# A head sum as two fp32r products, a later start for the last conv block, and output tiles finished one by one, in a one-core hybrid block

## The chip, the core and the metric

The kernel runs on one core of one Trainium2 chip, as one launch. The metric is the device time of that core in microseconds (us). The engines are TensorE (PE in the profile, with its weight loads as PEld), VectorE (DVE), ScalarE (ACT), GpSimd (POOL) and the DMA queues that SyncE (SP) starts. All arithmetic is in float32 or in fp32r, a rounded float32 format in which TensorE multiplies. An exact float32 operand is turned into two fp32r ones: a rounded copy ("hi") and the rest ("lo" = value minus hi).

## The reference, cut to what matters

```
h = rmsnorm(x) * (1 + scale) + shift                 # x: 2048 rows of 1024
p = h @ w_in                                         # value, gate, r, k, v, low-rank parts, output gates
# branch A: u = val*sigmoid(gate); causal depthwise conv of width 31; layernorm; swish; * silu(gate); @ w_conv_out
# branch B (RWKV-7), 16 heads of 64:
kk = (k * k_k).reshape(heads)
kk = kk / max(sqrt(sum(kk * kk, axis=-1)), 1e-12)    # the head sum that the change touches
o  = delta_rule_scan(r, decay, k, v, kk, kk * a)
y_rwkv = (groupnorm(o) + bonus) * silu(og) @ w_rwkv_out
out = (sigmoid(g_conv)*y_conv + sigmoid(g_rwkv)*y_rwkv) @ w_out
result = rmsnorm(x + gate * out, final_g)            # the end that the change touches
```

## The kernel before, in words

**Two phases.** Channels lie on the 128 partitions and 512 positions on the free axis, so a tile is 128x512. The 2048 positions are four blocks (b = 0 to 3). In the first phase each block runs `project` for every 128 columns of `w_in`: eight steps of three fp32r products (hi by hi, hi by lo, lo by hi). Between the projections lie the small products of the RWKV recurrence. A block has four slots (`slot`, g = 0 to 3), each with two pairs of heads (`pair`, line 998): 4 blocks x 8 pairs = 32 calls.

In the second phase blocks are taken two at a time ("s" = 0 and 1, the last pair of blocks being s = 1). For each, `wino` (line 1895) runs three Strassen-like products, in the order ro (RWKV output), co (conv output), o (the last projection). So `wino` is called six times, and `turn[0]` counts the calls. Each has seven part products, of four column tiles and 12 matmuls a tile. The part products are taken in the order 0, 4, 6, 2, 1, 3, 5 (0, 1, 6, 4, 2, 3, 5 in the first).

**Who sets the order.** The program is written out under `manual_schedule`: generators (`Task`) yield a time at which they may go on, and `poll` (line 223) lets them go on, the lowest rank first, as the emitted matmuls move the planner's clock `now`. `note` holds the planner's costs and due times. `ok(t)` is the time at which a tile is ready. `burst` (line 287) adds a lag of LAG = 1.0 us to it before a product is put into TensorE's queue. `idle("DVE", AHEAD)` lets a task wait until VectorE's planned work is less than 0.7 us ahead. Each engine then works through its own instructions in that order, and semaphores hold an instruction whose operand is late.

**The head sum** (lines 1043 to 1051, in `pair`). ScalarE squares k times k_k into `sq` (float32); one float32 product with `bones` (ones in two 64x64 blocks) sums over each head; ScalarE copies it to `ssr`; SP stores two rows of it to `dN`. Further on in the same generator come `y`, `BK`, `KR` and the masked products `As`, which the group's triangular inverse starts from. `dn` (the inverse of the squared norm) is read back from `dN`. A like sum stands further on: `rk` is split into `rh` and `s_lo`, and two fp32r products with `bones` follow.

**The conv branch of the last block.** The first three blocks' conv branches are finished in the first phase. The last block's layer norm ends in `last_norm` (`side[1]`), and `last_u` (line 2109), a task of rank 2, then takes the eight tiles one after the other: load `y` and the gate `co`, multiply by the inverse deviation, two ACT functions, two DVE products, store to `u_d`. It starts once `side[1]` is done and four cells of `uc` are free. The loads for the last co product wait until all eight are stored (`more_["u"]`).

**Lending buffers.** `lend_cells` (line 2077) hands buffers of the first phase to the second. At its end it loads `final_g` as a broadcast row `fg` (128x1024), then lends four weight slots and two raw weight slots, and lets six weight loads run ahead.

**The end** (`final`, line 2167, for each o product). Four output tiles of 128 rows for each of two blocks, each in two halves (h_ = 0, 1). VectorE adds x to the PSUM sum; ScalarE squares with an accumulated row sum into `sq8` (`square`); `finish(b_, ns)` waits until both halves of the rows `ns` are there, then runs on columns: mean plus epsilon, an integer first guess of the inverse root and three Newton steps of three operations, 12 small DVE operations in all; then one DVE multiplication by `rs` and `fg` and one store for each half tile. Before, `finish` is called once for the four tiles of block 0 (`finish(0, [0, 1, 2, 3])`), and for block 1 once, or four times with one tile each in the last pair. The last halves come in the order: block 1 with part product 3, block 0 with part product 5, the last one. All squares of a pair write the one tile `sq8`, and `finish` waits for `ok(sq)`.

Of the kernel before, what the change touches and what calls it, by code (L numbers as in the profile page):

```python
# [9 lines left out]
F32 = mybir.dt.float32  # L10
# [8 lines left out]
P = 128  # L19
# [63 lines left out]
def hybrid_block(ctx: ExitStack, tc: tile.TileContext, x, x_t, vecs, convk, w2a2, final_g, ada, w_in, w_co, w_ro, w_o, crow, out,  # L83
# [169 lines left out]
    def ok(*aps):  # L253
        ks = [key(a) for a in aps]
        return lambda: max(ready[q] for q in ks)
# [8 lines left out]
    def when(f):  # L264
        return lambda: 0.0 if f() else None
# [21 lines left out]
    def burst(*ws):  # L287
        w = both(*ws)

        def f():  # L290
            r = w()
            if r is None:
                return r
            return r + lag[0]

        return f
# [701 lines left out]
    def pair(G, q_, box):  # L998
# [41 lines left out]
        E1x = E1[:, :, 0:CH].rearrange("p (c e) t -> p c e t", e=2)  # L1040
        E1i = E1[:, :, 1:].rearrange("p (c e) t -> p c e t", e=2)
        E24 = E2.rearrange("p (c e t) -> p c e t", e=2, t=CH)
        sq = e1.tile([P, TB], F32, name="sq", tag="sq")
        nc.scalar.activation(sq, k, AF.Square, scale=vc("rwkv_k_k", pr))
        yield burst(ok(sq), free, bank("aux"))
        pss = pa.tile([P, TB], F32, name="aux", tag="aux")
        nc.tensor.matmul(pss, bones.bitcast(F32), sq, start=True, stop=True)
        ssr = e1.tile([P, TB], F32, name="ssr", tag="sq")
        nc.scalar.copy(ssr, pss)
        yield ok(ssr)  # L1050
# [680 lines left out]
    with tc.manual_schedule():  # L1731
# [345 lines left out]
        def lend_cells():  # L2077
            yield when(lambda: Gs[-2].chained)
            l3_cells(sc, "As", "As", "tk", "tk", "KR", "KR")
            yield when(lambda: Gs[-2].normed)  # L2080
            l3_cells(sc, "uv")
            yield when(lambda: Gs[-1].chained)
            l3_cells(sc, "KR", "KR")
            l3_cells(oc, "As", "As", "tk", "tk")
            yield when(lambda: Gs[-1].normed)
            wide[0] = 8
            l3_cells(oc, "uv")
            yield both(when(lambda: groups_[-1].done and side[0].done and side[1].done and len(mr[1][1].got) == 4),
                       hx.room(HXB - 4))
            for _ in range(HXB - 4):  # L2090
                fc.add(hx.take("fc"))
            late.close()
            sp = more_["sp"] = ctx.enter_context(tc.tile_pool(name="sp", bufs=1, reuse_waits="tile"))
            more_["fg"] = sp.tile([P, D], F32, name="fg")
            nc.sync.dma_start(more_["fg"], final_g.unsqueeze(0).broadcast_to([P, D]))
            wr.free.extend([now[0]] * NWX)
            wr.slots.extend([lambda name: sp.tile([P, KT, P], F32R, name=name, tag="wx", bufs=NWX)] * NWX)
            for t_ in slices(sp.tile([P, NRAWX, TB], F32, name="w_raw")):
                raws.add(t_)
            depth[0] = WB  # L2100
# [6 lines left out]
                    to.add(*slices(e2.tile([P, TB], F32, name="fc", tag=tag_, bufs=n_)))  # L2107

        def last_u():
            yield when(lambda: side[1].done)  # L2110
            yield uc.room(4)
            rl = uc.take()
            nc.sync.dma_start(rl, rl_d)
# [53 lines left out]
        def final(b0):  # L2167
# [4 lines left out]
                             for h_, b_, n in order_])  # L2172
            have = {}
            sp, fg = more_["sp"], more_["fg"]
            sq = sp.tile([P, 2, 4, 2], F32, name="sq8", tag="sq8", bufs=2)

            def plus(h_, b_, n, t_, ps):
                f = order_.index((h_, b_, n))
# [6 lines left out]
            class Done:  # L2185
# [10 lines left out]

                def square(self, h_, b_, n, t_, home):
                    yield ok(t_)
                    fsq = sp.tile([P, TB], F32, name="fsq", tag="fsq", bufs=2)
                    nc.scalar.activation(fsq, t_, AF.Square, accum_out=sq[:, b_, n, h_:h_ + 1])  # L2200
                    have[b_, n, h_] = t_, home

            def finish(b_, ns):
                m = len(ns)
                yield when(lambda: all((b_, n, h_) in have for n in ns for h_ in range(2)))
                vs, rs, rt = [sp.tile([P, 4], F32, name=n_, tag=n_, bufs=2)[:, :m] for n_ in ("vs", "rs", "rt")]
                yield both(ok(sq), idle("DVE", AHEAD))
                s_ = sq[:, b_, ns[0]:ns[0] + m, :]
                nc.vector.tensor_tensor(out=vs, in0=s_[:, :, 0], in1=s_[:, :, 1], op=ALU.add)
                nc.vector.tensor_scalar(out=vs, in0=vs, scalar1=1.0 / D, scalar2=RMS_EPS, op0=ALU.mult, op1=ALU.add)  # L2210
                rsqrt(rs, vs, None, nc.vector, rt)
                for i, n in enumerate(ns):
                    t0 = (b0 + b_) * TB + n * P
                    for h_ in range(2):
                        t_, home = have[b_, n, h_]
                        yield both(ok(t_, rs), idle("DVE", AHEAD))
                        nc.vector.scalar_tensor_tensor(out=t_, in0=t_, scalar=rs[:, i:i + 1],
                                                       in1=fg[:, h_ * TB:h_ * TB + TB], op0=ALU.mult, op1=ALU.mult)
                        nc.sync.dma_start(out[t0:t0 + P, h_ * TB:h_ * TB + TB], t_)
                        home.give(t_)  # L2220

            Task(finish(0, [0, 1, 2, 3]), 2)
            for ns in ([[0], [1], [2], [3]] if last else [[0, 1, 2, 3]]):
                Task(finish(1, ns), 2)
            return sums8(held(), held(), held(), Done(), plus)

        for c_, (m, s_) in zip(todo, seq_):
# [49 lines left out]
```

## Time and profile before

| What | Value |
|---|---|
| Median of 3 runs | 2690.75 us (2689.71 to 2692.74) |
| Profiled execution, its own time | 2690.07 us |
| Span of the profile (first to last instruction) | 2688.4 us |
| Mean granted TensorE clock | 0.989 |
| Matmuls | 18324 |
| VectorE instructions | 3658 |
| ScalarE instructions | 2306 |
| GpSimd instructions | 1817 |
| DMA | 712.11 MB, mean 265 GB/s |

Busy time is the share of the span in which an engine has an instruction under way; for TensorE it is rough, since matmuls overlap and their ends are modelled. So its pace is read from the starts of successive matmuls, not from the length of one. In a timeline row the first number is the start, the second the length, then engine, line, operation, output<-inputs, sizes and count, and in brackets the idle time before it and what ended that. Because all instructions are recorded in one helper, every line number reads L194, and tile names tell the operations apart.

### The profile page before, as it was taken

The page shows a single profiled execution, that of the slowest core. Times are in us where ns is not written, and L with a number is a line of the kernel's source. Part 1 is how long each engine was busy: PE and PEld are TensorE (multiplying, and loading weights), DVE is VectorE, ACT ScalarE, POOL GpSimd, SP SyncE. Part 2 cuts the span into 40 slices and gives each one's busy share as a digit, 9 for nine tenths or more (in the row PEclk, how much of TensorE's full clock was granted, in tenths as well). Part 3 has the DMA queues.
Part 4 walks back from the last instruction along what each step waited for, and adds up shares of the span by engine and source line. Part 5 has one row for each costly group of instructions (what it writes and reads, how often), then busy time and mean ns, then how long its engine had stood idle before and what let it go on. Part 6 is the DMA issues. An engine that isn't in the chain of part 4 may idle for free.

```text
span 2688.4 us, 50710 instructions
## 1 busy us (share of the span) xinstructions
PE 2589.7 (96%) x18324; PEld 2086.4 (78%) x18324; DVE 2178.6 (81%) x3658; ACT 1188.6 (44%) x2306; POOL 1315.4 (49%) x1817
## 2 busy tenths in 40 slices
PE   6999999999999999999999998999999988899997
PEld 5877888777877888888888877877887766688886
DVE  6786889788879887978698877878888699888586
ACT  5544444443434434434444333434344454455443
POOL 0576758562658383827573756492726593000000
PEclk9999999999999999999999999999999999999998
DMA  9788778787787688967876888686766779789884
GB/s 352 271 300 308 263 264 284 261 299 242 245 270 242 223 286 275 312 206 272 279 254 224 293 262 259 216 307 204 273 185 213 254 267 308 241 310 332 306 266 167
DMA packets 390835, 712.11 MB, mean 265 GB/s; under 512 B 137508, under 2 KB 141944, under 8 KB 390584
## 3 DMA queue, kind: packets, MB, share of 16 engines
q1 hardware_dynamic: 390584, 708.87, 78.0%
q8 instruction: 144, 2.36, 0.4%
q14 instruction: 107, 0.88, 0.1%
HBM read 494.34 MB, written 213.26 MB: 263 GB/s over the span
## 4 chain that ended last, share of the span: by engine, by line
PE 78%; DVE 10%; DMA 5%; POOL 3%; issue 2%; SPq 2%; ACT 1%; DVEq 0%; POOLq 0%; ACTq 0%
PE ps_main L194 63%; PE aux L194 6%; PE xo L194 5%; PE late L194 3%; SPq L194 2%; DVE As L194 1%; DMA w_lo<-kl_in 1%; DVE acc L194 1%; PE ps_f L194 1%; DVE gst L194 1%; DMA As<-dT 1%; DVE rs_t L194 1%; DVE h_lo L194 1%; DVE S L194 1%; DMA gr_d<-th 0%
## 5 line engine op out<-in xcount | busy, mean ns | idle before, releaser
L194 PE MATMUL ps_main<-h_hi,w_hi 128*128 128x512 f32 x2304 | 923.6, 401 | 8.0 <-DVE lora L194 4.7
L194 PE MATMUL ps_main<-h_hi,w_lo 128*128 128x512 f32 x2304 | 925.2, 402 | 5.0 <-POOL w_lo L194 2.9
L194 PE MATMUL ps_main<-h_lo,w_hi 128*128 128x512 f32 x2304 | 923.0, 401 | 0.0
L194 DVE SCALAR_TENSOR_TENSOR acc<-u,ck,acc 128x512 f32<-128x512 f32 x928 | 698.6, 753 | 26.7
L194 PEld LDWEIGHTS ps_main<-h_hi,w_hi 128*128 128x128 f32 x2304 | 435.1, 189 | 105.4 <-issue 6.7
L194 PEld LDWEIGHTS ps_main<-h_hi,w_lo 128*128 128x128 f32 x2304 | 435.1, 189 | 101.8 <-issue 5.7
L194 PEld LDWEIGHTS ps_main<-h_lo,w_hi 128*128 128x128 f32 x2304 | 435.1, 189 | 92.5 <-issue 5.0
L194 PE MATMUL ps_main<-h_hi,w_c 128*128 128x512 f32 x896 | 292.3, 405 | 10.5 <-DVE mr L194 3.6
L194 POOL TENSOR_TENSOR itmp<-La,TT 128x126 f32<-128x126 f32 (+22 forms) x496 | 207.0, 417 | 46.3 <-issue 13.2
L194 ACT ACTIVATE th<-ps_main 128x512 f32<-128x512 f32 x160 | 95.6, 598 | 285.8 <-PE ps_main L194 264.7
L194 POOL TENSOR_TENSOR TT<-TT,itmp 128x126 f32<-128x126 f32 (+22 forms) x496 | 202.1, 407 | 38.9
L194 PEld LDWEIGHTS ps_main<-h_hi,w_c 128*128 128x128 f32 x896 | 172.7, 193 | 53.0 <-ACT h_hi L194 4.2
L194 POOL TENSOR_TENSOR w_lo<-w_st,w_hi 128x1024 fp32r<-128x1024 f32 x55 | 133.4, 2425 | 140.1 <-ACT w_hi L194 125.0
L194 PE MATMUL ps_main<-h_lo,w_c 128*128 128x512 f32 x448 | 182.4, 407 | 14.0 <-DVE h_lo L194 12.2
L194 ACT COPY uv<-xo 64x256 f32<-64x256 f32 (+1 forms) x192 | 80.9, 438 | 208.9 <-PE xo L194 153.8
L194 DVE SCALAR_TENSOR_TENSOR S<-xo,pe,Se 64x64 f32<-64x64 f32 x512 | 123.1, 280 | 49.2 <-PE xo L194 37.9
L194 ACT CAST w_c<-w_raw 128x512 fp32r<-128x512 f32 x168 | 102.3, 619 | 93.1 <-DMA w_raw<-wk_o 33.9
L194 PE MATMUL ps_main<-w_c,h_hi 128*128 128x512 f32 x448 | 140.3, 394 | 0.0
L194 DVE TENSOR_TENSOR As<-aux,maskA 128x512 f32<-128x512 f32 x128 | 82.3, 684 | 47.5 <-PE aux L194 46.9
L194 PEld LDWEIGHTS ps_main<-h_lo,w_c 128*128 128x128 f32 x448 | 86.8, 194 | 37.2 <-DVE h_lo L194 15.4
L194 ACT ACTIVATE Se<-S,pe 128x128 f32<-128x128 f32 x256 | 88.7, 395 | 40.0 <-DVE S L194 38.7
L194 ACT ACTIVATE t<-ps_main,mu 128x512 f32<-128x512 f32 x96 | 65.9, 686 | 80.0 <-PE ps_main L194 79.6
(294 smaller groups left out, 4508.7 us busy)
## 6 DMA issues: line engine op xcount, KB each, us to landing
w_hi<-kh_in SPq DMA_DIRECT2D x219, 512.0 KB
w_lo<-kl_in SPq DMA_DIRECT2D x219, 512.0 KB
w_st<-w_in_t SPq DMA_DIRECT2D x73, 512.0 KB
kh_in<-w_hi SPq DMA_DIRECT2D x71, 512.0 KB
kl_in<-w_lo SPq DMA_DIRECT2D x71, 512.0 KB
lny<-y_d SPq DMA_DIRECT2D x80, 256.0 KB
w_raw<-wk_o SPq DMA_DIRECT2D x56, 256.0 KB
ada_st<-ada_t SPq DMA_DIRECT2D x16, 512.0 KB
```

Of the source, the lines that this page charges most:

```text
L194: r = f(*a, **k)
```

## The change

**The head sum.** The square `sq` goes into another buffer; ScalarE makes a rounded copy `sqh` (fp32r); VectorE takes the rest `sql`; the one float32 product becomes two fp32r products with `bones`. **The conv branch.** `last_u` also waits until `turn[0] >= 2`, the call of the second `wino` (co of the first pair of blocks). **The end.** `fg` is multiplied once by -1/256 on ScalarE, and `lend_cells` waits for its load first. In the last pair each of the eight tiles has its own small square-sum tile and its own `finish`, with eight small operations in place of 12 (the constants are folded into `fg`). In the first pair the four tiles stay together, with one operation more. `finish` tasks of block 1 are put in ahead of block 0. `fsq` has one buffer in place of two.

```diff
@@ in pair
-        sq = e1.tile([P, TB], F32, name="sq", tag="sq")
+        sq = e1.tile([P, TB], F32, name="sq", tag=YT)
         nc.scalar.activation(sq, k, AF.Square, scale=vc("rwkv_k_k", pr))
-        yield burst(ok(sq), free, bank("aux"))
+        sqh = e1.tile([P, TB], F32R, name="sqh", tag="sq")
+        yield ok(sq)
+        nc.scalar.copy(sqh, sq)
+        sql = e1.tile([P, TB], F32R, name="sql", tag=RHT)
+        yield ok(sqh)
+        nc.vector.tensor_tensor(out=sql, in0=sq, in1=sqh.bitcast(F32), op=ALU.subtract)
+        yield burst(ok(sql), free, bank("aux"))
         pss = pa.tile([P, TB], F32, name="aux", tag="aux")
-        nc.tensor.matmul(pss, bones.bitcast(F32), sq, start=True, stop=True)
+        nc.tensor.matmul(pss, bones, sqh, start=True, stop=False)
+        nc.tensor.matmul(pss, bones, sql, start=False, stop=True)
@@ in lend_cells
             nc.sync.dma_start(more_["fg"], final_g.unsqueeze(0).broadcast_to([P, D]))
+            yield ok(more_["fg"])
+            nc.scalar.mul(more_["fg"], more_["fg"], -1.0 / 256)
             wr.free.extend([now[0]] * NWX)
@@ in last_u
-            yield when(lambda: side[1].done)
+            yield when(lambda: side[1].done and turn[0] >= 2)
@@ in final
-            sq = sp.tile([P, 2, 4, 2], F32, name="sq8", tag="sq8", bufs=2)
+            if last:
+                sq = [[sp.tile([P, 1, 2], F32, name="sqn", tag="sqn", bufs=8) for _ in range(4)] for _ in range(2)]
+            else:
+                s8 = sp.tile([P, 2, 4, 2], F32, name="sq8", tag="sq8", bufs=1)
+                sq = [[s8[:, b_, n:n + 1, :] for n in range(4)] for b_ in range(2)]
@@ in square
-                    fsq = sp.tile([P, TB], F32, name="fsq", tag="fsq", bufs=2)
-                    nc.scalar.activation(fsq, t_, AF.Square, accum_out=sq[:, b_, n, h_:h_ + 1])
+                    fsq = sp.tile([P, TB], F32, name="fsq", tag="fsq", bufs=1)
+                    nc.scalar.activation(fsq, t_, AF.Square, accum_out=sq[b_][n][:, 0, h_:h_ + 1])
@@ in finish
-                yield both(ok(sq), idle("DVE", AHEAD))
-                s_ = sq[:, b_, ns[0]:ns[0] + m, :]
-                nc.vector.tensor_tensor(out=vs, in0=s_[:, :, 0], in1=s_[:, :, 1], op=ALU.add)
-                nc.vector.tensor_scalar(out=vs, in0=vs, scalar1=1.0 / D, scalar2=RMS_EPS, op0=ALU.mult, op1=ALU.add)
-                rsqrt(rs, vs, None, nc.vector, rt)
+                yield both(ok(sq[b_][ns[0]]), idle("DVE", AHEAD))
+                s_ = s8[:, b_] if m > 1 else sq[b_][ns[0]]
+                if m > 1:
+                    nc.vector.tensor_tensor(out=vs, in0=s_[:, :, 0], in1=s_[:, :, 1], op=ALU.add)
+                    nc.vector.tensor_scalar(out=vs, in0=vs, scalar1=1.0 / D, scalar2=RMS_EPS, op0=ALU.mult, op1=ALU.add)
+                    rsqrt(rs, vs, None, nc.vector, rt)
+                    nc.vector.tensor_scalar(out=rs, in0=rs, scalar1=-256.0, scalar2=None, op0=ALU.mult)
+                else:
+                    nc.vector.tensor_scalar(out=vs, in0=s_[:, :, 0], scalar1=s_[:, 0, 1:2], scalar2=D * RMS_EPS, op0=ALU.add,
+                                            op1=ALU.add)
+                    nc.vector.tensor_scalar(out=rs.bitcast(I32), in0=vs.bitcast(I32), scalar1=-0.5, scalar2=float(0x5F3759DF),
+                                            op0=ALU.mult, op1=ALU.add)
+                    for z_ in (3.0, 12.0, 768.0):
+                        nc.vector.tensor_scalar(out=rt, in0=rs, scalar1=rs, scalar2=vs, op0=ALU.mult, op1=ALU.mult)
+                        nc.vector.tensor_scalar(out=rs, in0=rt, scalar1=z_, scalar2=rs, op0=ALU.subtract, op1=ALU.mult)
@@ at the end of final
-            Task(finish(0, [0, 1, 2, 3]), 2)
-            for ns in ([[0], [1], [2], [3]] if last else [[0, 1, 2, 3]]):
-                Task(finish(1, ns), 2)
+            for b_ in (1, 0):
+                for ns in ([[0], [1], [2], [3]] if last else [[0, 1, 2, 3]]):
+                    Task(finish(b_, ns), 2)
```

## The prediction, made before the change was run

> **What bounds the kernel now.** I read the page's busy times first, then its chain of work, then the busy time by stage.
>
> ```profile
> span 2688.4 us, 50710 instructions
> PE 2589.7 (96%) x18324; PEld 2086.4 (78%) x18324; DVE 2178.6 (81%) x3658; ACT 1188.6 (44%) x2306; POOL 1315.4 (49%) x1817
> PE 78%; DVE 10%; DMA 5%; POOL 3%; issue 2%; SPq 2%; ACT 1%; DVEq 0%; POOLq 0%; ACTq 0%
> ```
>
> TensorE is busy for 96% of the span and holds 78% of the chain that ends last. So an instruction taken from TensorE should shorten the span, if it lies where TensorE does not wait. The windows view tells where that is. Its columns: the window and its length, then busy us and instructions of PE, PEld, DVE, ACT and POOL, then clock, DMA share and GB/s.
>
> ```profile
> 56.00:600.00 544.00, 535.07 (x3714) 430.77 (x3715) 436.61 (x672) 267.18 (x485) 356.90 (x440) 0.99 0.81 281
> 600.00:1130.00 530.00, 525.05 (x4084) 424.42 (x4083) 445.52 (x752) 215.59 (x436) 298.96 (x433) 1.00 0.79 262
> 1130.00:1640.00 510.00, 504.20 (x3963) 408.45 (x3962) 411.11 (x697) 212.96 (x433) 291.94 (x453) 1.00 0.78 256
> 1640.00:2090.00 450.00, 439.90 (x3296) 354.03 (x3295) 371.45 (x613) 173.57 (x346) 246.24 (x358) 1.00 0.72 235
> 2090.00:2200.00 110.00, 101.44 (x1179) 80.22 (x1179) 87.27 (x159) 56.88 (x118) 76.64 (x98) 1.00 0.75 254
> 2200.00:2260.00 60.00, 48.24 (x226) 36.41 (x225) 52.47 (x78) 23.51 (x44) 41.15 (x28) 0.89 0.89 293
> 2260.00:2350.00 90.00, 79.70 (x329) 62.84 (x328) 78.80 (x129) 44.09 (x77) 0.00 (x0) 0.95 0.81 274
> 2673.00:2689.00 16.00, 0.00 (x0) 0.00 (x0) 11.37 (x36) 0.72 (x2) 0.00 (x0) 0.55 0.48 180
> ```
>
> The first four rows are the first phase. TensorE idles there for 8.9 + 5.0 + 5.8 + 10.1 = 29.8 us of 2034, or 1.5%: it is the bound. The next three rows are the handover between the phases: 8.6 + 11.8 + 10.3 = 30.7 us idle in 260, with VectorE busy for 87% in the second and 88% in the third; what binds there is VectorE, the loads and the order together. The last row is the tail: TensorE has nothing left and VectorE works alone. All 32 head sums lie in the first phase, `last_u` starts in the handover, and the single tiles lie in the tail.
>
> **The head sum.** Around one of the 32, the timeline of TensorE says:
>
> ```profile
> 2059.04 0.40 PE L194 MATMUL ps_main<-h_lo,w_hi 128*128 128x512 f32 x1
> 2059.28 1.02 PE L194 MATMUL aux<-sq,bones 128*128 128x512 f32 x2
> 2059.73 0.79 PE L194 MATMUL ps_main<-h_hi,w_lo 128*128 128x512 f32 x1
> 2060.36 0.39 PE L194 MATMUL ps_main<-h_hi,w_hi 128*128 128x512 f32 x1
> 2060.59 0.40 PE L194 MATMUL ps_main<-h_lo,w_hi 128*128 128x512 f32 x1
> ...
> 454.95 0.40 PE L194 MATMUL aux<-rh,bones 128*128 128x512 f32 x1
> 455.19 0.39 PE L194 MATMUL aux<-s_lo,bones 128*128 128x512 f32 x1
> 455.42 0.39 PE L194 MATMUL ps_main<-h_lo,w_hi 128*128 128x512 f32 x1
> ```
>
> Projections start 0.23 us apart (2060.36 to 2060.59). The float32 product is two records, and from its start to that of the second projection behind it 1.08 us pass (2059.28 to 2060.36), one projection included: 1.08 - 0.23 = 0.85 us. The new form is in the trace already: the two fp32r products of the other head sum, with the same ones matrix, take 455.42 - 454.95 = 0.47 us. Each head sum gives back 0.85 - 0.47 = 0.38 us, and 32 of them 12.2 us.
>
> Added are 32 rounded copies on ScalarE and 32 subtractions on VectorE. Their nearest rows (the list of groups; the last number before the bar is the count, behind it busy us and mean ns) and the ones that show how long such a VectorE operation can take:
>
> ```profile
> L194 ACT CAST rh<-rk 128x512 fp32r<-128x512 f32 x32 | 19.8, 618 | 51.4 <-DVE rk L194 51.3
> L194 DVE TENSOR_TENSOR h_lo<-mr,h_hi 128x512 fp32r<-128x512 f32 x40 | 26.7, 684 | 8.8 <-ACT h_hi L194 8.7
> L194 DVE TENSOR_TENSOR h_lo<-hf,h_hi 128x512 fp32r<-128x512 f32 x40 | 33.0, 854 | 7.9 <-ACT h_hi L194 7.7
> ...
> L194 DVE SCALAR_TENSOR_TENSOR y<-ta,k x32: 674/689/2425, 83.4 to 2060.2; 128x512 f32<-128x512 f32 x32
> ...
> PE aux L194 <- ACT sq L194: 0.5, 1, 0.5
> ```
>
> ScalarE gets 32 x 0.62 = 19.8 us, VectorE 32 x 0.68 to 0.85 = 22 to 27 us. The first phase hides both: VectorE was idle for 369 us of those 2034 (2034 - 436.61 - 445.52 - 411.11 - 371.45), ScalarE for more, and VectorE's filling work there, the conv taps, only moves up. Gone this cover, the price would be the whole 22 to 27 us.
>
> What may not be hidden is a wait. The two new steps lengthen the way from the square to the product by 1.3 us, plus up to 0.7 us of taps queued on VectorE. The product is put into TensorE's queue only 1.0 us after the planner thinks `sql` ready. If VectorE is later than that, TensorE, which works in order, waits with the projections queued behind it. Before, this wait came once, for 0.5 us in all (last row). VectorE operations in the first phase can be late: `y` has a median of 0.69 us but a maximum of 2.43. The bounds are 0 (none late) and 32 x (2.43 - 0.69 - 1.0) = 24 us (all as late as the slowest `y`). I take 1.5 us, two such waits, near the row of 0.5: a maximum against a median that close to the minimum (674 and 689) means few are slow.
>
> The subtractions beside a busy GpSimd took 854 ns (`h_lo<-hf`), those of the last stage, where POOL's column is 0, took 684 (`h_lo<-mr`). The Trainium skill, page "GPSIMD Engine Reference", section "1. Specifications", says that GpSimd shares its SBUF interfaces with VectorE and contends with VectorE instructions that have two SBUF inputs, as the new subtraction has; the trace agrees in sign. By that rule GpSimd's chain of the last group would end about 0.7 to 0.9 us later, which would make the total below 0.7 to 0.9 us smaller.
>
> Buffers: `sq` and `sql` go into the buffers of `y` and `rh`, whose readers have finished in the pair before; cost nothing. Behind the new waits in the generator stand `ssr`, the two stores to `dN`, `y`, `BK` and `KR`, all 1.3 to 2 us later in each pair. No TensorE work is put in before they are ready, so only the last group's chain, which reaches into the handover, can pass this on.
>
> **The handover.** Four edits meet here: the last pair's later chain, the start of `last_u`, the wait for `fg`, and its scaling.
>
> ```profile
> 2251.96 0.43 SPq L194 DMA_DIRECT2D fg<-final_g  x1
> ...
> 2255.07 0.68 DVE L194 TENSOR_TENSOR fc<-fc 128x512 f32<-128x512 f32 x1
> ...
> 2269.64 0.59 ACT L194 COPY cells<-ps_main 128x512 f32<-128x512 f32 x1 [1.05 <-PE ps_main L194]
> ...
> 2434.74 0.32 SPq L194 DMA_DIRECT2D u_d<-fc  x1
> ...
> ACT w_c L194 <- DMA w_raw<-w_ro_t: 6.9, 1, 6.9
> ```
>
> The co product's first column of 12 matmuls is copied out at 2269.64, so it began near 2269.6 - 12 x 0.23 = 2266.8, and that is when `turn[0]` becomes 2. The first tile of `last_u` was multiplied on VectorE at 2255.07, so it moves some 15 us on. Its three loads leave the crowded SP queue and DMA of 2200 to 2260 (DMA share 0.89) and three VectorE operations of 0.68 us leave the stretch where VectorE binds, to fall on one hardly less busy. Its last store, 2434.74, moves to about 2450; the co product that reads it is the fifth of six, and from the last matmul, 2672.7, back over two calls of 336 x 0.23 = 77 us it begins near 2518. That gap of 68 us is the cover. Gain or loss: at most the three operations, 2 us, either way; I take -0.5. `lend_cells` now lends the weight slots only once `fg` has landed, up to 6.9 us later if this load waits like the slowest one above, while the ring's older slots carry on: 0 to 6.9 us, taken as 0.5, since TensorE ran on after that place. The scaling is one ScalarE operation of twice 0.62 us in a stage where ScalarE is busy for 24 of 60. The later last chain: 0 to 2 us, taken as 0.5. Together +0.5.
>
> **The tail.** VectorE's timeline, from the first of the last eight tiles to be completed, and the last store:
>
> ```profile
> 2653.32 0.69 DVE L194 TENSOR_TENSOR cells<-ps_main,cells 128x512 f32<-128x512 f32 x1 [0.30 <-PE ps_main L194]
> 2654.86 0.16 DVE L194 TENSOR_TENSOR vs<-sq 128x1 f32<-128x1 f32 x1 [0.85 <-ACT fsq L194]
> ...
> 2672.72 0.69 DVE L194 TENSOR_TENSOR fc<-ps_main,fc 128x512 f32<-128x512 f32 x1 [1.35 <-PE ps_main L194]
> ...
> 2673.99 0.15 DVE L194 TENSOR_TENSOR vs<-sq 128x1 f32<-128x1 f32 x1
> ...
> 2676.17 0.16 DVE L194 TENSOR_TENSOR vs<-sq 128x4 f32<-128x4 f32 x1
> ...
> 2678.43 2.07 DVE L194 SCALAR_TENSOR_TENSOR cells<-cells,rs,fg 128x512 f32<-128x512 f32 x3
> ...
> 2684.39 0.74 DVE L194 SCALAR_TENSOR_TENSOR fc<-fc,rs,fg 128x512 f32<-128x512 f32 x1
> ...
> 2685.16 0.33 SPq L194 DMA_DIRECT2D out<-fc  x1
> ```
>
> Behind the last sum (2672.72) come 12 small operations for one tile of block 1 (2673.99 to 2676.17, 0.18 us each), 12 for all of block 0, and ten multiplications from 2678.43 to 2685.13 (0.66 each). Singly, a tile costs VectorE one sum, 0.65, eight small operations, 8 x 0.18 = 1.46, and two multiplications, 1.32: 3.43 us. Sums come every 12 x 0.23 = 2.8 us, so VectorE cannot keep up and becomes the bound of the last 30 us: 2653.32 + 0.85 (the one wait for a square) + 8 x 3.43 = 2681.6, against 2685.13. That gains 3.5 us; I take 3.4, for a gap or two. If the waits of before come again it is 0. With an idle VectorE the last tile alone would end at 2672.72 + 1.54 + 1.46 + 1.32 = 2677.0, a gain of 8.1, which the work queued excludes. The last store took 2688.4 - 2685.16 = 3.2 us to the end of the span, behind nine others 0.66 us apart; I let that stand. In the first pair, one small operation more, the new order of the tasks and the single `fsq` lie under a busy TensorE; nothing.
>
> **The sum.** -12.2 + 1.5 + 0.5 - 3.4 = -13.6 us. The profiled execution took 2690.07 us, 0.68 below the median of 2690.75; so 2676.5 for a profile and 2677.2 us for the median. About 0.2%, 5.4 us, is what a measurement of this kernel can tell from no change.
>
> **The rivals.** (1) The handover comes out worse. The planner's order there follows its own clock, and everything before it moves; for it speaks that its 30.7 us of waits have a dozen releasers, against it that the edits take work out of the crowded stretch. If a third of those waits comes on top, 10.2 us: 2677.2 - 0.5 + 10.2 = 2686.9, with smaller shares from 2682 on. (2) TensorE is not the bound in the first phase, and its saving becomes idle time: only the tail is left, 2690.75 - 3.4 = 2687.4. Against it: the starts 0.23 us apart on both sides of the head sum. The Trainium skill, page "Perfetto Trace Analysis", section "Identifying the Most-Contended Engine", speaks for it: matmul busy time is a bad measure of how near TensorE is to its limit, and the share of weight loads, here 78%, a better one. (3) Slower: VectorE is late to the subtraction nearly every time, and TensorE stands still for it. The saving of 12.2 + 3.4 us is eaten when the mean wait per head sum passes 15.6 / 32 = 0.49 us; at the 24 us bound above it gives 2690.75 - 15.6 + 24 = 2699.2. For it speaks VectorE's 81%; against it that one wait of 0.5 us in 32. That the products would not become cheaper can be left out: the same pair of products stands in the trace.
>
> **How the numbers follow.** My forecast, 2677.2 with its own 2669 to 2682, has a chance of 0.73; rival 1 has 0.15, rival 2 0.07, rival 3 0.05. The low end is all terms at their good ends: -12.2 - 3.5 and 6 of the handover's 30.7 us gone, 2669. The high end, 2686, takes in the waits at 4 us with the handover 6 us worse and 2 us off the tail's gain (-12.2 + 4 + 6 - 1.4 = -3.6, 2687), less its outer edge. Faster by over 0.2% (below 2685.4): the forecast and most of rival 1, 0.85. Within 0.2%: the rest of it and rival 2, 0.1. Slower: rival 3, 0.05.
>
> **What would show it.** Right: `aux<-sqh,bones` and `aux<-sql,bones` start 0.23 us apart and the next projection 0.47 after the first; TensorE's waits for `sql` sum to under 4 us; the first phase ends some 11 us sooner, at about 2079 in place of 2090; from the last matmul to the end 12 to 13 us in place of 15.7, with VectorE hardly idle in the last 25. Wrong: waits of `aux` for DVE `sql` of a third of a microsecond and more each; the windows of the handover with over 36 us idle; or a first phase no shorter although its matmuls are.

## The result: 0.6% slower, and the profile after

The changed kernel took 2708.3 us (median of 19 runs, 2696.7 to 2716.2), the kernel before, beside it on the same chip, 2692.2 us (19 runs, 2686.7 to 2702.5). The ratio is 1.0059 (95% interval 1.0048 to 1.0069): some 16 us slower, where 13.6 less were predicted. The profiled execution of the changed kernel is the slowest of its 19 (2716.2 us), so its parts show where the time went, and some 8 us too much of it. The profile before lies 2.1 us below its median, so the two profiles are 26 us apart and the medians 16.

The page of the changed kernel, busy times and chain:

```profile
span 2714.5 us, 50812 instructions
PE 2588.8 (95%) x18324; PEld 2088.5 (77%) x18324; DVE 2199.3 (81%) x3684; ACT 1209.8 (45%) x2339; POOL 1338.3 (49%) x1829
PE 21%; DVE 4%; DMA 2%; POOL 1%; issue 1%; SPq 0%; ACT 0%; DVEq 0%; POOLq 0%; ACTq 0%
```

TensorE is busy for as long as before (2589.7), in a span 26 us longer. The chain could be followed back through only 29% of the span this time, so the windows have to say where. Their columns are those of the prediction:

```profile
56.00:600.00 544.00, 522.85 (x3629) 421.19 (x3630) 424.82 (x658) 265.38 (x483) 343.25 (x425) 0.98 0.79 271
600.00:1130.00 530.00, 523.02 (x4080) 424.70 (x4079) 449.23 (x763) 221.67 (x445) 301.89 (x451) 1.00 0.79 260
1130.00:1640.00 510.00, 500.68 (x3952) 405.14 (x3951) 408.54 (x682) 214.10 (x430) 289.35 (x417) 1.00 0.79 260
1640.00:2090.00 450.00, 438.22 (x3295) 354.88 (x3294) 383.55 (x633) 184.34 (x366) 266.65 (x389) 0.99 0.73 237
2200.00:2260.00 60.00, 54.64 (x396) 42.75 (x394) 47.77 (x78) 31.72 (x68) 59.94 (x42) 1.00 0.82 268
2260.00:2350.00 90.00, 77.71 (x307) 60.34 (x307) 78.32 (x117) 41.09 (x71) 20.19 (x14) 0.91 0.80 270
2698.00:2715.00 17.00, 0.00 (x0) 0.00 (x0) 12.69 (x36) 0.72 (x2) 0.00 (x0) 0.64 0.41 154
```

TensorE stood still in the first phase for 49.2 us of 2034 (29.8 before), 21.2 of it in the first row, where it did 3629 matmuls instead of 3714. GpSimd, which was through with its work by 2260 before, still has 20.19 us of it in the second-last row; what that work is stands below, with the handover.

The edit itself did what it says. TensorE's timeline around one head sum, and what the trace answers for the tile `sql` (minimum, median and maximum in ns; the second line is how long VectorE sat idle ahead of the subtraction, waiting for `sqh`, and how often; the third the same of TensorE ahead of the product, waiting for `sql`):

```profile
2081.80 0.39 PE L194 MATMUL ps_main<-h_hi,w_lo 128*128 128x512 f32 x1
2082.03 0.40 PE L194 MATMUL aux<-sqh,bones 128*128 128x512 f32 x1
2082.27 0.39 PE L194 MATMUL aux<-sql,bones 128*128 128x512 f32 x1
2082.50 0.39 PE L194 MATMUL ps_main<-h_hi,w_hi 128*128 128x512 f32 x1
2082.72 0.39 PE L194 MATMUL ps_main<-h_lo,w_hi 128*128 128x512 f32 x1
```

```profile
L194 DVE TENSOR_TENSOR sql<-sq,sqh x32: 673/685/2644, 83.8 to 2080.2; 128x512 fp32r<-128x512 f32 x32
  ACT sqh L194: 11.0, 4
  DVE sql L194: 0.4, 1
```

From the first product's start (2082.03) to the next projection's (2082.50) are 0.47 us. VectorE stood 11.0 us in all (four times) at the head of its queue for `sqh`, and TensorE 0.4 us for `sql`.

To compare kernels I number TensorE's matmuls into `ps_main`: all kernels have 8,928. "First phase" is from the start of the 1st to that of the 6,722nd; "head sums" is what 32 stretches of it take, each from the start of the projection ahead of a head sum to that of the second one behind it (so each holds two projections); "rest" is the first phase without them; "handover" is from the 6,721st to the 7,729th; "tail" from the start of the last to the end of the span. (The kernel's own first phase has 6,912 of them; its last 192 are counted with the handover here.) All in us, from one profiled execution each:

| | head sums | rest | handover | tail | span |
|---|---|---|---|---|---|
| before | 44.4 | 1978.9 | 315.1 | 16.1 | 2688.4 |
| after | 33.8 | 2004.7 | 326.4 | 17.2 | 2714.5 |
| difference | -10.6 | +25.8 | +11.3 | +1.1 | +26.1 |

The predicted saving is there, and 2.4 times as much is lost in the rest of the same phase (the columns leave out -1.4 us ahead of the first matmul and between handover and tail). This is the sign of being wrong that the prediction had named last: a first phase no shorter although its matmuls are. The experiments below are read by the same columns. A profiled execution can lie some way from its kernel's median (from 8.8 us below it in a_sem14 to 10.5 above in blind_all), so the parts show where time goes, and the medians how much.

### The profile page after: what moved, and what is told of

Read it like the earlier page. It is cut to its first block, busy times and chain, and to the rows that moved or that the text cites. A ratio compares the mean times of both kernels' runs of the same rounds, so it can differ in the third digit from the quotient of the medians.

```text
span 2714.5 us, 50812 instructions
## 1 busy us (share of the span) xinstructions
PE 2588.8 (95%) x18324; PEld 2088.5 (77%) x18324; DVE 2199.3 (81%) x3684; ACT 1209.8 (45%) x2339; POOL 1338.3 (49%) x1829
## 5 line engine op out<-in xcount | busy, mean ns | idle before, releaser
L194 POOL TENSOR_TENSOR TT<-TT,itmp 128x126 f32<-128x126 f32 (+22 forms) x496 | 207.9, 419 | 38.9
L194 PE MATMUL ps_main<-h_lo,w_c 128*128 128x512 f32 x448 | 181.6, 405 | 14.7 <-DVE h_lo L194 11.1
```

The source lines that it names most:

```text
L194: r = f(*a, **k)
```

## The experiments

Eighteen kernels ran, those of one group on one chip, each beside the kernel before (its medians there: 2691.7, 2691.6, 2693.8, 2693.1, 2691.6). The theory that I began with, **L**: the pair's generator is serial, `ssr` starts later behind the square (6.65 us after the square's end, 3.14 before, means of 32), and the next pair's copies out of PSUM wait for the end of the pair before. Rivals: **H**, the handover's edits; **W**, the added work itself; **O**, the order, which the planner builds from its own estimates of every duration. Below, "order" includes the engine: the planner gives some subtractions (`h_lo<-cells,h_hi` and `w_c<-w_raw,w_c`) to VectorE or to GpSimd, and the changed kernel has 13 more of these on GpSimd than the kernel before.

### Which part, and is it the edit at all?

**only_a**: the head sum of the diff alone. 

> The kernel before with the new head sum alone; `last_u`, `fg` and the tail stay as they were. Theory L (longer chain): the pair's generator is serial, the square now reaches `ssr` some 3.5 us later, the next pair's k, r and v tiles are taken from PSUM only when the pair before is done, and TensorE has two banks, so it stands still. Then the first phase ends 12 to 18 us later than before, as in the changed kernel, and the time is 2700 to 2710 us. Rival H (handover): the first phase's loss is small and the changed kernel lost its time to the wait for `fg` and to `last_u`. Then this one gains most of the predicted 12 us: 2679 to 2687 us.

Measured: 2709.5 us, ratio 1.0065 (1.0048 to 1.0083). Head sums 34.1, rest 2000.9, handover 326.1. The whole loss is the head sum's, the handover's too; H falls.

**no_a**: the diff without its head sum. 

> The changed kernel with the float32 head sum of before; `last_u`, `fg` and the tail stay changed. Theory L: the first phase is as before (TensorE's 6720th projection at about 2079 us); left are the wait for `fg`, some 6 us, and the tail, 1 us longer: 2692 to 2700 us. Rival H: 2705 to 2710 us, as the changed kernel.

Measured: 2683.9 us, ratio 0.9973 (0.9960 to 0.9986): faster than both kernels, and below both expectations. Rest 1980.7, handover 307.1, tail 17.2.

**own_split**: the head sum in a generator of its own; the pair goes on.

```diff
+        def head_sum():
+            sq = e1.tile([P, TB], F32, name="sq", tag="sq")
...
+        summed = Task(head_sum(), 2)
...
+        yield when(lambda: summed.done)
         rh = e1.tile([P, TB], F32R, name="rh", tag=RHT)
```

> The kernel before with the new head sum in a task of its own: the pair's generator goes straight on to `y` and BK and waits for the head sum only ahead of `rh`. The added copy, subtraction and products are all there. Theory L: the pair is no longer than before, so the saving of 32 x 0.38 us shows: 2676 to 2684 us, and VectorE's waits with its queue blocked for `sqh` cost nothing by themselves. Rival W (the work itself: an added VectorE operation that waits at the head of its queue for ScalarE, and holds the evacuations behind it): as slow as the kernel with the new head sum alone, 2700 us and more.

Measured: 2704.4 us, ratio 1.0039 (1.0025 to 1.0053). From the square's start to the end of GpSimd's `vv` are 35.6 us on average (37.2 before, 40.8 after), so the chain is no longer, and most of the loss is still there, as W expected: L falls as the main cause, and W or O is left.

**null_sem**: not a single instruction added or taken.

```diff
-SEM = 0.13
+SEM = 0.14
```

> The kernel before with one constant of its planner changed, the time it reckons for a semaphore 0.14 in place of 0.13 us; no instruction is added or taken. Theory L: the order shifts a little, 2686 to 2698 us. Rival O (order): the planner's order is so finely set that any change of its times costs as much as the change did: 2700 us and more.

Measured: 2706.3 us, ratio 1.0053 (1.0038 to 1.0068). Nearly the whole loss of the change, from 0.01 us in the planner's head. Taking the longest sequence that two programs have in common, this one has 1,511 of TensorE's 13,996 instructions (head sums left out) in another place than before; the kernel with the head sum alone has 1,477. The prediction never priced that.

### Order and work taken apart

**blind**: the new head sum in exactly the order of before. Copy, subtraction and products are issued past the planner's books (`tc.nc` in place of `nc`), which record the old product.

```diff
+        tc.nc.scalar.copy(sqh, sq)
...
+            tc.nc.vector.tensor_tensor(out=sql, in0=sq, in1=sqh.bitcast(F32), op=ALU.subtract)
...
-        nc.tensor.matmul(pss, bones.bitcast(F32), sq, start=True, stop=True)
+        tc.nc.tensor.matmul(pss, bones, sqh, start=True, stop=False)
+        tc.nc.tensor.matmul(pss, bones, sql, start=False, stop=True)
+        note("PE", "matmul", pss, [bones.bitcast(F32), sq])
```

> The kernel before with the new head sum, but the planner is not told of it: it goes on reckoning one float32 product behind the square, and the copy, the subtraction and the two products are issued beside its books. Every other instruction keeps exactly the place that it had before on each engine. Theory O (order): the change lost its time because the planner, fed with other durations, put some 1,500 of 13,996 TensorE instructions elsewhere. With the order of before the saving shows: 12.2 us less, given back in part where `sql` is late (0 to 8 us), 2680 to 2689 us. Rival W (the work itself): the added copy and subtraction hold up the evacuations on ScalarE and VectorE wherever they stand: 2700 us and more.

Measured: 2711.8 us, ratio 1.0066 (1.0046 to 1.0086). A miss for O as I had put it: the time is in W's range. TensorE's longest sum of waits, and its timeline at the longest single one:

```profile
PE aux L1059 <- DVE sql L1051: 16.1, 11, 4.2
```

```profile
427.35 0.39 PE L194 MATMUL ps_main<-h_hi,w_hi 128*128 128x512 f32 x1
427.58 0.40 PE L1058 MATMUL aux<-sqh,bones 128*128 128x512 f32 x1
432.22 0.79 PE L1059 MATMUL aux<-sql,bones 128*128 128x512 f32 x1 [4.24 <-DVE sql L1051]
432.81 0.63 PE L194 MATMUL ps_main<-h_lo,w_hi 128*128 128x512 f32 x1
433.24 0.63 PE L194 MATMUL ps_main<-h_hi,w_lo 128*128 128x512 f32 x1
```

Here the prediction's third rival did come true: with the product at its old place, TensorE waited 16.1 us for `sql`, and the head sums took 53.1 us. After the long wait projections start 0.43 us apart. So this run does not price the work alone; late_20 and work_only below come closer. In the diff the planner knows of the subtraction and puts the products later, which is why they waited 0.4 us there.

**phantom**: the order of only_a, no instruction moved, but the float32 product is issued, and no copy or subtraction (the edit is shown against only_a).

```diff
-        nc.scalar.copy(sqh, sq)
+        note("ACT", "copy", sqh, [sq], 0.0, [sq])
...
-        nc.tensor.matmul(pss, bones, sqh, start=True, stop=False)
-        nc.tensor.matmul(pss, bones, sql, start=False, stop=True)
+        tc.nc.tensor.matmul(pss, bones.bitcast(F32), sq, start=True, stop=True)
+        note("PE", "matmul", pss, [bones, sqh])
+        note("PE", "matmul", pss, [bones, sql])
```

> The reverse: the planner is told of the copy, the subtraction and the two fp32r products and orders everything as in the kernel with the new head sum alone (no instruction moved on any engine), but what is issued is the one float32 product of before; copy and subtraction are left out. The result is the reference's. Theory O: as slow as that kernel (2709.5 us) or slower by some of the 12.2 us that the float32 products take more: 2706 to 2722 us. Rival W: without the added work the time comes back, 2690 to 2696 us.

Measured: 2717.1 us, ratio 1.0092 (1.0068 to 1.0116); head sums 46.1, rest 2009.4. The work of before in the order of the change is 25 us slower than before; W cannot do that. (`sq` and `ssr` keep the buffers of the change here. In work_only below they stand in the old order, and buffers and added work together cost 4.6 us.) Within this order the new head sum may be worth its money, 2717.1 to 2709.5 us, but the intervals of the two ratios overlap.

**blind_all** (as blind, with the other two parts of the diff): 

> The changed kernel (`last_u`, `fg` and the tail as changed), its head sum split, but the planner told of the float32 product as in the run where it is not told: the order is that of the changed kernel with the float32 head sum, which took 2683.9 us. Theory O: that less the head sum's saving, 2672 to 2682 us, faster than both kernels. Rival W: 2692 us and more.

Measured: 2699.1 us, ratio 1.0029 (1.0014 to 1.0044); head sums 52.1. Again W's range: like blind it is slower than its partner with the float32 product, here by 15 us (no_a).

**a_sem14** (only_a with `SEM = 0.14`): 

> The kernel with the new head sum alone and the planner's semaphore time at 0.14 in place of 0.13 us, told of the new head sum. Theory O: a third order of the same work, somewhere among those seen, 2695 to 2715 us, and below null_sem's 2706.3 us by part of the 12.2 us saved if luck is equal. Theory L (longer chain): its loss comes on top of that of null_sem, 2715 us and more.

Measured: 2717.4 us, ratio 1.0086 (1.0066 to 1.0106), in L's range and above O's. See a_sem12, below.

### The order of before, with the products late enough

**late_20**: as blind, with products, `ssr` and its stores 2.0 us later.

```diff
+        def product():
+            yield after(2.0)
+            tc.nc.tensor.matmul(pss, bones, sqh, start=True, stop=False)
+            tc.nc.tensor.matmul(pss, bones, sql, start=False, stop=True)
+            tc.nc.scalar.copy(ssr, pss)
...
```

> As the run in which the planner is not told of the new head sum, but the two products, the copy to `ssr` and its two stores are issued 2.0 us later than there; every other instruction on TensorE, VectorE and GpSimd keeps the place that it had before. Theory S (stalls): that run lost its saving because TensorE stood at `sql` in 13 of 32 pairs for 20.9 us in all, and after the longer of these its next projections started 0.43 us apart in place of 0.23. 2.0 us later, some 4 us of those waits are left: the intervals with a head sum give back 8 us of the 10 that the kernel with the new head sum alone showed, and the time is 2682 to 2689 us. Rival W (the work itself): the 12 us that were lost away from the head sum come from the added copy and subtraction in full queues and stay: 2695 us and more.

Measured: 2695.4 us, ratio 1.0005 (0.9988 to 1.0021). One wait for `sql` is left, the second row (the first is TensorE's longest sum of waits here):

```profile
PE late L194 <- DVE Tn L194: 9.4, 5, 4.1
PE aux L1065 <- DVE sql L1051: 2.2, 1, 2.2
```

Head sums 33.3, a saving of 11.1; but the rest took 1994.8, 16 more (in the slowest execution of its 12, 7.0 us above the median). The time is at the lower edge of W's range: no gain.

**late_u** (the same with the later `last_u`): 

> The same, and `last_u` begins later, as in the change; the tail and `fg` as before. Theory S: the later `last_u` gains some 7 us in the handover beside the head sum's 4 to 8: 2674 to 2682 us, faster than every kernel so far. Rival W: 2688 us and more.

Measured: 2692.5 us, ratio 0.9998 (0.9983 to 1.0013). Head sums 33.9, rest 1985.3. Theory S expected too much again; the time is in W's range.

**only_last_u**: one line of the diff.

```diff
-            yield when(lambda: side[1].done)
+            yield when(lambda: side[1].done and turn[0] >= 2)
```

> The kernel before with `last_u` begun later alone. The changed kernel with the float32 head sum took 2683.9 us; its aligned trace gained 6.8 us between TensorE's 7392nd and 7728th projection, and lost 1 us in the tail. If the gain is that of `last_u`: 2682 to 2686 us. If it comes from the scaling of `fg` or the tail's new order: 2690 to 2693 us.

Measured: 2686.3 us, ratio 0.9979 (0.9966 to 0.9991). The later `last_u` gains by itself, 5.7 us by the ratio (2.4 to 9.2). It moves 5 of TensorE's instructions, all behind the first phase.

**only_tail**: the diff's parts in `lend_cells` (`fg`), `square` and `finish` alone. 

> The kernel before with the scaling of `fg` and the single tiles of the last pair alone; no place on TensorE or GpSimd moves. The tail costs VectorE eight small operations of 0.21 to 0.27 us for each of eight tiles in place of 12 each for five groups: from the last matmul to the end 16.7 to 17 us in place of 15.7, as in the changed kernel. If the wait for `fg` delays the weights' slots, the co product starts up to 6 us later. 2690 to 2699 us; the prediction had a gain of 3.4 us in the tail, 2687 to 2689 us.

Measured: 2692.0 us, ratio 1.0001 (0.9981 to 1.0021), tail 17.2, handover 315.6 (before 315.1). In this order the wait for `fg` costs nothing that shows, and the tail gains nothing. VectorE's timeline in the tail of this kernel shows why, with one tile's eight small operations and the multiplication behind them:

```profile
2676.40 0.20 DVE L194 TENSOR_SCALAR vs<-sqn 128x1 f32<-128x1 f32 x1
2676.63 0.15 DVE L194 TENSOR_SCALAR rs<-vs 128x1 int32<-128x1 int32 x1
2676.82 0.27 DVE L194 TENSOR_SCALAR rt<-rs,vs 128x1 f32<-128x1 f32 x1
2677.13 0.21 DVE L194 TENSOR_SCALAR rs<-rt,rs 128x1 f32<-128x1 f32 x1
...
2678.25 0.21 DVE L194 TENSOR_SCALAR rs<-rt,rs 128x1 f32<-128x1 f32 x1
2678.38 0.74 DVE L194 SCALAR_TENSOR_TENSOR cells<-cells,rs,fg 128x512 f32<-128x512 f32 x1
```

From 2676.40 to 2678.38 are 1.98 us, 0.25 us each, where I had put 0.18, the pitch of operations with constants or whole operands. An operation that reads two values per partition (`rt<-rs,vs`) took 0.27 us and 0.31 to the next.

### The saving alone and the work alone

**mm_only**: the saving without the work; the rest of the square is left out.

```diff
-        sq = e1.tile([P, TB], F32, name="sq", tag="sq")
+        sq = e1.tile([P, TB], F32R, name="sq", tag="sq")
...
-        nc.tensor.matmul(pss, bones.bitcast(F32), sq, start=True, stop=True)
+        for _ in range(2):
+            tc.nc.tensor.matmul(pss, bones, sq, start=True, stop=True)
...
```

> The kernel before in its own order, with the saving alone: the square is written as fp32r, and its product is two fp32r matmuls of the same rounded part, the second overwriting the first; the rest's part of the computation is left out, and with it copy and subtraction. The planner still reckons one float32 product. Theory E (added work costs elsewhere): TensorE's 32 head sums take 11 to 12 us less and the time falls by that, 2679 to 2683 us. Rival N (TensorE's time is worth nothing in the first phase, since the groups' chain on VectorE and GpSimd sets the pace): 2689 to 2694 us.

Measured: 2685.5 us, ratio 0.9979 (0.9963 to 0.9995). Head sums 31.9, 12.5 less; the rest took 1988.3, 9.4 more, with no work added and nothing moved (of which the two executions, 3.2 us above the median here and 2.1 below it before, may make some 5). By the ratio 5.7 us of 12.5 arrive (1.3 to 10.0): about half, between E and N, and not all.

**work_only**: the work without the saving.

```diff
+        tc.nc.scalar.copy(sqh, sq)
...
+            tc.nc.vector.tensor_tensor(out=sql, in0=sq, in1=sqh.bitcast(F32), op=ALU.subtract)
...
         nc.tensor.matmul(pss, bones.bitcast(F32), sq, start=True, stop=True)
```

> The reverse: the rounded copy on ScalarE and the subtraction on VectorE are issued as in the run in which the planner is not told, but nothing reads them; the product is the float32 one of before, in its place. Every other instruction keeps its place. Theory E: 8 to 15 us slower than before, 2700 to 2707 us. Rival N: no change, 2690 to 2695 us.

Measured: 2696.2 us, ratio 1.0017 (1.0001 to 1.0033): 4.6 us, less than E expected. Rest 1989.6, in an execution 7.9 us above the median.

**sub_pool**: late_20 with the subtraction on GpSimd.

```diff
-            tc.nc.vector.tensor_tensor(out=sql, in0=sq, in1=sqh.bitcast(F32), op=ALU.subtract)
+            tc.nc.gpsimd.tensor_tensor(out=sql, in0=sq, in1=sqh.bitcast(F32), op=ALU.subtract)
```

> As late_20 (order of before, products 2.0 us later), with the subtraction on GpSimd in place of VectorE. If it is VectorE's share of the added work that costs: 4 to 10 us below late_20's 2695.4, 2685 to 2691 us. If it is the ScalarE copy, or GpSimd's chain of 31 steps suffers as much: 2693 to 2700 us.

Measured: 2698.6 us, ratio 1.0022 (1.0003 to 1.0040). No better than late_20: taking the subtraction off VectorE gains nothing.

**null_12**: the kernel before with the constant moved the other way.

```diff
-SEM = 0.13
+SEM = 0.12
```

> The kernel before with the planner's semaphore time at 0.12 in place of 0.13 us; nothing else. Theory O (the order of before is one of the better ones, and nearly any other costs): 2697 to 2712 us. Rival: null_sem was bad luck, and this is 2686 to 2694 us.

Measured: 2727.1 us, ratio 1.0129 (1.0103 to 1.0156), 34 us slower, more than any other run and more than theory O had room for (its range ended at 2712). Handover 339.0. TensorE's longest wait in the first phase, first of null_12 and then of the changed kernel (timelines), with the clock of the latter (windows):

```profile
108.01 0.60 PE L194 MATMUL aux<-ident,vv 128*128 128x128 f32 x4
113.84 0.80 PE L194 MATMUL ps_main<-h_hi,w_hi 128*128 128x512 f32 x1 [5.23 <-DVE k L194]
114.43 0.63 PE L194 MATMUL ps_main<-h_lo,w_hi 128*128 128x512 f32 x1
114.86 0.63 PE L194 MATMUL ps_main<-h_hi,w_lo 128*128 128x512 f32 x1
```

```profile
107.66 0.60 PE L194 MATMUL aux<-ident,vv 128*128 128x128 f32 x4
113.68 0.80 PE L194 MATMUL ps_main<-h_hi,w_hi 128*128 128x512 f32 x1 [5.42 <-DVE k L194]
114.27 0.63 PE L194 MATMUL ps_main<-h_lo,w_hi 128*128 128x512 f32 x1
114.70 0.63 PE L194 MATMUL ps_main<-h_hi,w_lo 128*128 128x512 f32 x1
```

```profile
108.00:113.60 5.60, 0.26 (x3) 0.02 (x1) 0.79 (x2) 4.11 (x9) 3.56 (x2) 0.87 0.83 275
113.70:118.50 4.80, 4.80 (x11) 3.82 (x12) 0.75 (x1) 0.48 (x2) 1.02 (x3) 0.50 0.53 177
```

The largest single wait that the change brought in the first phase, 5.4 us for `k`, is in null_12 as well, with the old head sum: it belongs to the order. And it costs twice: at a clock of 0.50 the next 4.80 us hold 11 projections, where the pace of 0.23 us would make 21.

**a_sem12** (only_a with `SEM = 0.12`): 

> The kernel with the new head sum alone and the planner's semaphore time at 0.12 in place of 0.13 us. Theory O (the order rules, the head sum itself is worth about nothing): anywhere between 2695 and 2730 us, with no regard to null_12's 2727. Rival L (the longer chain costs in any order): 2730 us and more, since it was 11 to 18 us above its partner in the two other pairs.

Measured: 2701.7 us, ratio 1.0037 (1.0021 to 1.0052), 25 us below its partner null_12, where L had it at 2730 and more. L falls for good.

**null_ahead**: another constant of the planner, in the kernel before.

```diff
-AHEAD = 0.7
+AHEAD = 0.72
```

> The kernel before with the time that the planner lets VectorE's queue run ahead at 0.72 in place of 0.70 us; nothing else, and TensorE's order is the same for its first 8,949 of 13,996 instructions. Theory O, if the loss goes with what is moved: 2694 to 2702 us. If the order of before is nothing special: 2687 to 2695 us.

Measured: 2700.8 us, ratio 1.0032 (1.0018 to 1.0045), with 448 instructions moved on TensorE. Its rest took 1975.5 us, as before; the handover 329.3.

| planner's `SEM` | float32 head sum | split head sum |
|---|---|---|
| 0.12 | 2727.1 | 2701.7 |
| 0.13 | 2692 (before) | 2709.5 |
| 0.14 | 2706.3 | 2717.4 |
| mean | 2708.5 | 2709.5 |

Over three orders the split head sum is worth nothing that can be told from their scatter. Of the orders that differ from it within the first phase, none that ran is as good as that of before: null_sem, null_12, null_ahead, only_a, own_split, a_sem14 and a_sem12 are seven others of the same work, with the old or the new head sum, and lie 9 to 34 us above it. (Only_last_u, whose order differs behind the first phase alone, is faster.)

## Why the prediction was wrong

**The term of the edit was right.** Products 0.23 us apart, TensorE's waits for `sql` 0.4 us (predicted under 4), and the head sums 10.6 us shorter, where -12.2 + 1.5 had been predicted; with waits of 0.4 in place of 1.5 the saving itself was about 11.0, so the close agreement of the sums is in part luck. Rival 3 did not happen in the changed kernel; blind shows what would have made it happen.

**The step that failed** is the one that kept everything else in place: "No TensorE work is put in before they are ready, so only the last group's chain, which reaches into the handover, can pass this on", and the subtractions whose cover "only moves up". The planner puts each instruction where its own clock says, and the new durations of the head sum alone moved 1,477 TensorE instructions, from the first pair on. Phantom prices that by itself, without any of the new work: 25 us. Null_sem, null_12 and null_ahead price the same thing with no change at all: 15, 34 and 9 us. I had seen the mechanism ("the planner's order there follows its own clock"), but only for the handover, with 10.2 us at most and a chance of 0.15, and as if a new order could only vary about the old one. The old one was far better than its neighbours, which a trace of it cannot show; one run with a planner's constant changed would have.

**The saving was priced at its full length**, and even in the old order it is not worth that. mm_only: 12.5 us off TensorE, about 5.7 off the time (1.3 to 10.0). The second rival is borne out by half: TensorE's 96% did not make it the bound in every microsecond. The Trainium skill (page "Perfetto Trace Analysis", section "Identifying the Most-Contended Engine") says that matmul busy time misjudges how near TensorE is to its limit; mm_only agrees. Where the other half went is not shown: the rest of the phase took 9.4 us more, but in one profiled execution each, and four kernels of the same order and work there differ by 7 us (1976.5 to 1983.4).

**The added work was put at nothing** ("the first phase hides both"); alone in the old order it cost 4.6 us (0.3 to 8.9). Saving, work and the last wait for `sql` make -5.7 + 4.6 + 2.2 = +1.1 us, and late_20 measured 1.0005. So without the order's loss the new head sum would have been about even. In the new order the parts do not close: 25 for the order (phantom), 8 less for the new head sum in it (not clear of noise) and 7 less for the other edits (no_a) make 10 of the 16 us measured.

**The handover** was predicted at +0.5 and lost 11.3, of which only_a has 11.0: again the order. The rows show one thing that goes with it. In the changed kernel the planner gave GpSimd 20 `h_lo<-cells,h_hi` and 27 `w_c<-w_raw,w_c` in place of 13 and 21. One takes GpSimd some 1.5 us and VectorE 0.7. GpSimd's last instruction, behind which `lend_cells` loads `fg` (2 to 6 us later in every trace), came 36 us later, where the first phase ended 15 us later (before, then after):

```profile
2248.76 1.62 POOL L194 TENSOR_TENSOR oc<-oc,zr 128x512 f32<-128x512 f32 x1 [1.10 <-DMA zr<-ro_d]
```

```profile
2285.10 1.62 POOL L194 TENSOR_TENSOR oc<-oc,zr 128x512 f32<-128x512 f32 x1
```

Over the 20 traces the handover is longer the later this instruction starts, counted from the 6,721st projection: 169 to 177 us go with a handover of 307 to 323 us, 182 to 191 with 318 to 326, 196 to 210 with 329 to 339. No run tried this by itself, and null_sem is late (187 us) with only two such subtractions more on GpSimd. `last_u` was undersized: -0.5 predicted, 5.7 us gained where the order around it stays. The wait for `fg` cost nothing that shows in the old order (only_tail); in the changed kernel it stands on the chain of waits:

```profile
2290.30 7.20 DMA fg<-final_g
```

The load was issued at 2290.30 and ended a step of the chain 7.20 us later; whether that cost the changed kernel anything was not tried by itself.

**The tail** was predicted at -3.4 and came out at +1.1. VectorE was the bound there, as predicted (12.69 us busy in the last 17 us, of which 3 lie behind its last instruction). The mis-sized term is the small operation: 0.25 us, not 0.18; over eight tiles 8 x (1.98 - 1.46) = 4.2 of the 4.5 us missed.

What stays open: which property makes the order of before so much better. In the first phase the losses of the others are spread over dozens of waits. no_a, the diff without its head sum, is the fastest complete kernel that ran.

## What to carry to other kernels

Where a planner or scheduler orders the instructions by estimated durations, an edit can change the order of everything behind it, and that can weigh more than the edit: here 9 to 34 us against 12. Measure a null edit first (one planner constant by a hair), and price the edit in a frozen order, by hiding it from the planner, and over several orders. A saving on the busiest engine is worth its length only where nothing else ends at the same time; test it alone, without the work that pays for it.

## What the runs showed of the hardware

TensorE's granted clock fell to 0.50 after long waits, as in the rows above: projections 0.43 us apart in place of 0.23. In the first phases of all 20 traces there are 109 such slow spells of four projections and more; they lasted 2 to 5 us, most often 3. Counting gaps from one TensorE start to the next there, 13 of 14 of over 4 us were followed within 9 us by at least four projections at that pace, 18 of 30 between 3 and 4 us, 34 of 79 between 2 and 3, 19 of 102 between 1.5 and 2, and 7 of 135 between 1 and 1.5. Of gaps between 2 and 3 us that had no other of 1 us and more near them (12 us ahead, 9 behind), it is 28 of 63. The page "TensorE: Matmul & The Clock Gate" of the Trainium skill, Part 1, has this as a window of about 3.4 us: an idle one halves the clock. The traces agree in the factor, and show waits well under 3.4 us followed by it too. The wait of 5.4 us above thus cost 11 x 0.20 = 2.2 us more, and an edit that brings a few such waits can lose more than their sum.
